# A hybrid SSD, RG-LRU, GLA and HGRN decoder step: transposes, scores, norm order and decay copies rearranged

## The chip, the cores and the metric

One core of one Trainium2 chip runs the whole program. The metric is the device time of one execution in microseconds (us). The kernel before took 1928.42 us, the median of 3 runs from 1928.1 to 1928.71 us.

## What is computed

Two layers of a decoder trunk on 592 tokens: 16 meta tokens, 8 sample sequences of 8 tokens, and a prompt of 512. Every product is in fp32.

```python
D_MODEL = 1024; D_FF = 4096; SEQ = 512; DEC_BATCH = 8; DEC_SEQ = 8; N_META = 16
# layer 0: 16 SSD heads (2 groups, head 64, state 128) and an RG-LRU (8 blocks of 128)
# layer 1: 4 GLA heads (key 128, value 256) and 8 HGRN heads (128, 128)
for layer in range(2):
    mixed = mixer(h)                       # one combined input projection, the heads, one output projection
    h = layer_norm(ALPHA * h + mixed)      # ln1
    h = layer_norm(ALPHA * h + square(relu(h @ w1)) @ w2)   # ln2
# SSD, per chunk:  y = (cb * decay) @ xd + (C @ S) * exp(b);   S = S * exp(b_last) + B.T @ (xd * to_end)
# GLA and HGRN:    scores = (q exp(b - b_ref)) @ (k exp(b_ref - b)).T, masked causal, times v, plus q exp(b) @ S
```

## The kernel before

Activations lie with features on partitions and tokens along the free axis: a tile "h" is one of eight slices of 128 features, 592 tokens wide, worked on in two halves of 296 (288 behind the last output projection). An fp32 product is made of three reduced-precision matmuls. `parts` casts a weight unit of 128x1024 to its high part on ScalarE (L126) and takes the low part by a subtraction on VectorE (L127); `mm` (L182) then runs k over the eight slices with three matmuls each, 24 matmuls for one 128x296 result in one of five PSUM banks ("pm"). `fast_pair` (L195) does half of the MLP's second product with fewer multiplications. Weight units are prepared three ahead of their use (`next_unit`, `prep_to`).

A `Task` is one weight unit with its result for both halves. The side work (heads, norms) is written as generators on a list `active`; `weave` advances each of them by one stage after every half task, and `later[k]` holds pieces that are to run inside the next product behind its k-th slice. So the order of the program text on the five engines comes from where a generator yields, and a scheduler settles the last details; every engine then executes its own instructions in order. The side work has three PSUM banks of its own ("px").

The parts that the change touches:

- **The norm** (class `Norm`). The last product in front of a norm has five slices without and three with the norm's sums woven in. `add` (L427 to L447) gives a slice's square to ScalarE (L446), adds it to the sum of squares "lnq" on VectorE (L447), and the slice itself to the sum "lns" (on POOL, for the last slice on VectorE, L444). `finishing` sums over partitions by two products with ones (L463, L465), makes the reciprocal deviation, subtracts the mean (L478), scales (L494) and writes the next layer's "h" as high part (ScalarE, L495) and low part (VectorE, L496). The first half's `finishing` starts inside the second half's first product behind slice FIK = 3; the second half's comes after everything that is pending has been drained.
- **The first product after a norm** runs its first four tasks by halves, each task with all of its k in turn (`run(..., by_half=True)`, L648 in the MLP; L1404 in the odd mixer, whose first task is a narrow one, L247).
- **The convolution** (`conv_task`, L689; 12 slices for SSD, 8 for RG-LRU): ScalarE moves the product out of PSUM into "pad" (L697 to L702), VectorE multiplies the first tap (L706) and adds the other three (L708 and the caller's).
- **An SSD pair** (`pair`, L831; 8 pairs of heads, two half tasks to a stage): POOL multiplies the log decays, high and low part, into a triangular mask (L843, 128x1024 each, and L845, 128x160 each); TensorE sums them along the chunk, ScalarE exponentiates (L881, L885). States follow (L903 to L925), "yi" = C S (L925) times its decay on VectorE, and then the outputs: L942 adds "yi" into the output bank as a product with the identity, L945 and L948 add the intra-chunk part.
- **A GLA or HGRN head** (`attend`): the decayed keys "kx" are laid out for four chunks of 128 tokens in three pieces of 64 (L1178 to L1203), and the scores are eight products of 64 columns (L1265, L1266), a full one of 128 keys for each half chunk of queries.

```python
            run([w1(0, f) for f in W1_ORDER[:4]], by_half=True)
    def finish(self, i, dst):
        if i == 0:
            later.setdefault(FIK, []).append(lambda: step(self.finishing(i, dst)))
```

## Time and profile before

| what | value |
|---|---|
| median of 3 runs | 1928.42 us |
| the profiled execution's own time | 1926.06 us |
| its span in the trace | 1924.3 us |
| mean granted TensorE clock | 0.987 of full speed |
| TensorE matmuls (PE) | 1858.2 us busy, 97% |
| VectorE (DVE) | 1297.1 us, 67% |
| ScalarE (ACT) | 886.0 us, 46% |
| GpSimd (POOL) | 417.2 us, 22% |

The profiled execution took 1.76 us more than its span, and 2.36 us less than the median of the three runs. The rows further down are from its trace. In a row of instructions the fields are the start in us, the time from the start of the first to the end of the last in us, engine, line, operation, output and inputs, shape and count; in brackets stands the time the engine idled before it and whose result ended the idling. A product in fp32 (all of L463, L942, L1265 and their like) appears as two matmul records, a reduced-precision one or a transpose as one. [...]

### The profile page before, as it was taken

The page shows a single profiled execution, that of the slowest core. Times are in us where ns is not written, and L with a number is a line of the kernel's source. Part 1 is how long each engine was busy: PE and PEld are TensorE (multiplying, and loading weights), DVE is VectorE, ACT ScalarE, POOL GpSimd, SP SyncE. Part 2 cuts the span into 40 slices and gives each one's busy share as a digit, 9 for nine tenths or more (in the row PEclk, how much of TensorE's full clock was granted, in tenths as well). Part 3 has the DMA queues.
Part 4 walks back from the last instruction along what each step waited for, and adds up shares of the span by engine and source line. Part 5 has one row for each costly group of instructions (what it writes and reads, how often), then busy time and mean ns, then how long its engine had stood idle before and what let it go on. Part 6 is the DMA issues. An engine that isn't in the chain of part 4 may idle for free.

```text
span 1924.3 us, 33593 instructions
## 1 busy us (share of the span) xinstructions
PE 1858.2 (97%) x13854; PEld 1819.0 (95%) x13854; DVE 1297.1 (67%) x2035; ACT 886.0 (46%) x1550; POOL 417.2 (22%) x435
## 2 busy tenths in 40 slices
PE   8998899999999999998999999999999999999996
PEld 8998799899999999998999999999999999999996
DVE  7997766877975756549645465665755976666647
ACT  5333246623644444324644455665732653534333
POOL 2554432214100000035422222221203200000024
PEclk9999899999999999999999999999999999999998
DMA  6232221421213131322332233223231214141311
GB/s 205 91 114 72 75 100 47 132 88 47 87 56 120 46 127 48 122 76 72 132 113 104 100 104 106 84 90 102 91 126 56 77 56 132 46 131 55 122 55 50
DMA packets 68761, 175.97 MB, mean 91 GB/s; under 512 B 6624, under 2 KB 30304, under 8 KB 67456
## 3 DMA queue, kind: packets, MB, share of 16 engines
q1 hardware_dynamic: 67968, 171.40, 26.5%
q8 instruction: 109, 1.79, 0.4%
q0 software_dynamic: 640, 2.43, 0.4%
q14 instruction: 44, 0.36, 0.1%
HBM read 154.54 MB, written 19.25 MB: 90 GB/s over the span
## 4 chain that ended last, share of the span: by engine, by line
PE 80%; DVE 13%; ACT 3%; issue 3%; POOL 0%; DMA 0%; SPq 0%; ACTq 0%; DVEq 0%; POOLq 0%
PE pm L182 55%; PE pm L195 14%; DVE w L127 1%; DVE r L424 1%; DVE h L496 1%; DVE r L494 1%; PE px L1326 1%; DVE r L478 1%; PE px L1337 1%; PE px L1336 1%; PE px L1067 1%; DVE lnq L447 1%; DVE acc L708 1%; PE px L925 1%; DVE ln L447 1%
## 5 line engine op out<-in xcount | busy, mean ns | idle before, releaser
L182 PE MATMUL pm<-h,w 128*128 128x296 f32 (+2 forms) x8256 | 1178.2, 301 | 11.0 <-ACT h L308 5.4
L182 PEld LDWEIGHTS pm<-h,w 128*128 128x128 f32 x8256 | 1132.6, 189 | 22.6 <-ACT h L308 5.4
L127 DVE TENSOR_TENSOR w<-raw,w 128x1024 fp32r<-128x1024 f32 (+1 forms) x300 | 369.7, 1233 | 165.1 <-ACT w L126 164.5
L126 ACT CAST w<-raw 128x1024 fp32r<-128x1024 f32 (+1 forms) x300 | 304.2, 1015 | 301.6 <-PE pm L195 152.2
L195 PE MATMUL pm<-ff,w 128*128 128x296 f32 (+1 forms) x2016 | 273.3, 297 | 0.0
L195 PEld LDWEIGHTS pm<-ff,w 128*128 128x128 f32 x2016 | 271.9, 188 | 0.1
L620 POOL TENSOR_TENSOR sq<-sq 128x296 f32<-128x296 f32 (+1 forms) x32 | 21.5, 674 | 651.4 <-ACT sq L618 651.4
L182 PE MATMUL pm<-m,w 128*128 128x296 f32 (+1 forms) x768 | 108.2, 304 | 0.0
L182 PE MATMUL pm<-ff,w 128*128 128x296 f32 (+1 forms) x768 | 108.0, 303 | 0.0
L182 PEld LDWEIGHTS pm<-m,w 128*128 128x128 f32 x768 | 106.8, 194 | 0.8 <-issue 0.3
L182 PEld LDWEIGHTS pm<-ff,w 128*128 128x128 f32 x768 | 106.6, 193 | 0.8 <-issue 0.3
L607 DVE TENSOR_TENSOR ff<-sq,ff 128x888 fp32r<-128x888 f32 (+3 forms) x48 | 58.4, 1221 | 42.1 <-ACT ff L606 42.1
L588 ACT ACTIVATE sq<-pm 128x296 f32<-128x296 f32 (+1 forms) x96 | 37.9, 414 | 87.0 <-PE pm L182 66.0
L606 ACT CAST ff<-sq 128x888 fp32r<-128x888 f32 (+3 forms) x48 | 50.3, 1050 | 39.6 <-DVE sq L601 38.9
L1361 POOL TENSOR_TENSOR o<-o,zs 128x576 f32<-128x576 f32 x16 | 31.3, 1967 | 148.7 <-DVE o L1360 148.7
L1280 POOL TENSOR_TENSOR sin<-sin,ebl 128x1024 f32<-128x1024 f32 (+1 forms) x12 | 35.8, 2980 | 106.1 <-issue 101.2
L211 DVE TENSOR_TENSOR r<-r,pm 128x296 f32<-128x296 f32 (+1 forms) x96 | 43.5, 453 | 18.6 <-PE pm L195 18.0
L589 ACT ACTIVATE sq<-sq 128x296 f32<-128x296 f32 (+1 forms) x96 | 41.2, 450 | 0.8
L1366 ACT COPY v<-pm 128x296 f32<-128x296 f32 x32 | 12.9, 405 | 58.6 <-PE pm L182 58.6
L214 DVE TENSOR_TENSOR r<-r,pm 128x296 f32<-128x296 f32 (+1 forms) x72 | 32.6, 452 | 10.2 <-PE pm L195 10.2
L618 ACT ACTIVATE sq<-pm 128x296 f32<-128x296 f32 (+1 forms) x32 | 13.0, 414 | 56.8 <-PE pm L182 53.8
L495 ACT ACTIVATE h<-r,vec 128x296 fp32r<-128x296 f32 (+1 forms) x48 | 23.8, 536 | 31.5 <-DVE r L494 31.5
(390 smaller groups left out, 2261.3 us busy)
## 6 DMA issues: line engine op xcount, KB each, us to landing
raw<-in_w_dram SPq DMA_DIRECT2D x252, 512.0 KB, 3.3
sin<-in_sst_dram SPq DMA_DIRECT2D x8, 512.0 KB, 3.7
out_ssd_s_dram<-sin SPq DMA_DIRECT2D x8, 512.0 KB, 3.1
sin<-in_gst_dram SPq DMA_DIRECT2D x4, 1024.0 KB, 5.7
out_gla_s_dram<-sin SPq DMA_DIRECT2D x4, 1024.0 KB, 3.9
sin<-in_hst_dram SPq DMA_DIRECT2D x8, 512.0 KB, 4.4
out_hgrn_s_dram<-sin SPq DMA_DIRECT2D x8, 512.0 KB, 3.5
xt<-in_x_dram SPq DMA_DIRECT2D x16, 148.0 KB, 4.2
```

What stands on the lines that cost most here:

```text
L126: A.copy(w[:, 0, :n], r)
L127: V.tensor_tensor(w[:, 1, :n], r, w[:, 0, :n].bitcast(F32), OP.subtract)
L182: PE.matmul(p[:, :n], w[:, a, ks], xs[k][:, b, c0:c1], start=(k == 0 and i == 0), stop=(k == KT - 1 and i == 2))
L195: PE.matmul(p[:, :n], w[:, a, ks], xs[k][:, b, :n], start=(first and k == 0 and i == 0), stop=(k == 3 and i == 2), skip_group_check=True)
L211: V.tensor_tensor(y, y, p[:, :n], OP.add)
L214: V.tensor_tensor(y, y, p[:, :n], OP.subtract)
L447: V.tensor_tensor(ss, ss, q, OP.add)
L588: A.activation(q, p, AF.Relu)
L589: A.activation(q, q, AF.Square)
L606: A.copy(t[:, 0, a:e, :n], s[:, a + 1:e + 1, :n])
L607: V.tensor_tensor(t[:, 1, a:e, :n], s[:, a + 1:e + 1, :n], t[:, 0, a:e, :n].bitcast(F32), OP.subtract)
L1280: G.tensor_tensor(sin, sin, ebl[:, 0:8].unsqueeze(2).to_broadcast([P, 8, N]), OP.mult)
```

## The change

Line numbers of the changed kernel are up to 53 higher. In six places:

1. A new function `together` takes the first four tasks behind a norm, opens their four PSUM banks at once and runs k on the outside: slice k is multiplied into all four results before slice k+1 is needed. The MLP's first four W1 tasks and the first GLA head's first four tasks use it for the first half; the second half runs in two groups of two.
2. In the norm the first half's `finishing` starts behind slice 6 instead of 3; the addition of a square waits until the next slice has been added (`add_square`); and before the second half's drain the next four weight units are prepared.
3. The convolution's first tap goes from VectorE (L706) to ScalarE, as an activation with scale and bias from a column.
4. The SSD log decays are no longer multiplied on POOL; ScalarE writes them as 20 copies for each pair with a scale per partition (16 of 128x128, 4 of 128x80), in three batches.
5. The product that adds "yi" into the outputs is marked as a transpose.
6. The scores are four products of 128 columns and four of 64 keys by 64 columns; "kx" becomes one run of 576 columns plus 256, so that the pieces of VectorE and ScalarE work around it are fewer; where a head has two value slices (GLA, `nv` == 2) the sample products move ahead of the scores.

```diff
 SHK = 5
-FIK = 3
+FIK = 6
 FINY = (2, 4, 6)
...
             self.consume(p, c0, c1, i)
+            flush()
+            weave()
+    def together(tasks, i):
+        ps = []
+        for t in tasks:
+            if t.small is None and t.w is None:
+                t.w = next_unit()
+            ps.append(pm())
+        for k in range(KT):
+            ks = slice(k * P, (k + 1) * P)
+            for t, p in zip(tasks, ps):
+                c0, c1 = t.halves[i]
+                if t.small is not None:
+                    ops = [(p[:32], t.small[:, k, :], b) for b in range(2)]
+                else:
+                    ops = [(p, t.w[:, a, ks], b) for a, b in ((0, 0), (0, 1), (1, 0))]
+                for j, (o, w, b) in enumerate(ops):
+                    PE.matmul(o[:, :c1 - c0], w, t.xs[k][:, b, c0:c1], start=(k == 0 and j == 0),
+                              stop=(k == KT - 1 and j == len(ops) - 1))
+            for fn in later.pop(k, ()):
+                fn()
+        for t, p in zip(tasks, ps):
+            c0, c1 = t.halves[i]
+            t.consume(p[:32 if t.small is not None else P, :c1 - c0], c0, c1, i)
             flush()
...
             self.new = new
+            self.square = None
...
             A.activation(q, r, AF.Square)
-            V.tensor_tensor(ss, ss, q, OP.add)
+            self.add_square()
+            self.square = (ss, q)
+        def add_square(self):
+            if self.square:
+                ss, q = self.square
+                V.tensor_tensor(ss, ss, q, OP.add)
+            self.square = None
...
             else:
+                prep_to(state["use"] + 4)
                 drain()
...
         def finishing(self, i, dst):
+            self.add_square()
             c0, c1 = self.halves[i]
...
-            run([w1(0, f) for f in W1_ORDER[:4]], by_half=True)
+            ts = [w1(0, f) for f in W1_ORDER[:4]]
+            together(ts, 0)
+            together(ts[:2], 1)
+            together(ts[2:], 1)
             for k, f in enumerate(W1_ORDER[4:]):
...
                 acc = cp.tile([P, PW], F32, tag="acc", name="acc")
-                V.tensor_scalar(acc[:, 0:OW], t[:, 0:OW], w(0), b, OP.mult, OP.add)
+                A.activation(acc[:, 0:OW], t[:, 0:OW], AF.Identity, scale=w(0), bias=b)
                 for k in (1, 2):
...
             rx = s1.tile([P, 2, 2, 80], F32R, tag="rx", name="rx")
-            for i, l in enumerate((lah.bitcast(F32), lal.bitcast(F32))):
-                G.tensor_tensor(rr[:, i], l[:, 1:5, hh].unsqueeze(3).to_broadcast([P, 4, 2, P]),
-                                umask[:, None, None, :].to_broadcast([P, 4, 2, P]), OP.mult)
-                G.tensor_tensor(rx[:, i], l[:, 0, hh].unsqueeze(2).to_broadcast([P, 2, 80]),
-                                uxmask[:, None, 0:80].to_broadcast([P, 2, 80]), OP.mult)
+            def decays(m):
+                for i, l in enumerate((lah.bitcast(F32), lal.bitcast(F32))):
+                    for h in range(2):
+                        def scaled(out, mask, c):
+                            A.activation(out, mask, AF.Copy, scale=l[:, c, 2 * j + h:2 * j + h + 1])
+                        if m == 2:
+                            scaled(rx[:, i, h], uxmask[:, 0:80], 0)
+                        else:
+                            for c in (2 * m, 2 * m + 1):
+                                scaled(rr[:, i, c, h], umask, c + 1)
+            decays(0)
             xr = s1.tile([P, 2, 3, 40], F32, tag="xr", name="xr")
...
             yield
+            decays(1)
+            decays(2)
             xd = s2.tile([P, 5, 2, 64], F32, tag="xd", name="xd")
...
                 PE.matmul(q[:, c * P:(c + 1) * P], yi[:, c].rearrange("p h q -> p (h q)"), ident,
-                          start=(c == 0), stop=False, skip_group_check=True)
+                          start=(c == 0), stop=False, is_transpose=True, skip_group_check=True)
             for h in range(2):
...
-            kx = sd.tile([P, 64 + 4 * 192], F32, tag="kx", name="kx")
-            kc = kx[:, 64:].rearrange("p (c r s) -> p c r s", c=4, r=3)
+            kx = sd.tile([P, 576 + 256], F32, tag="kx", name="kx")
+            k2 = kx[:, 576:].rearrange("p (c s) -> p c s", c=4)
             for o, s, r in zip(chunks(e1, 64), chunks(bs, 64), (4, 32)):
...
             b4 = chunks(bs, 128)[1]
-            V.tensor_tensor(kc[:, :, 1], b4[:, :, 96:97].to_broadcast([P, 4, 64]), b4[:, :, 0:64], OP.subtract)
+            V.tensor_tensor(k2, b4[:, :, 96:97].to_broadcast([P, 4, 64]), b4[:, :, 0:64], OP.subtract)
             c = slice(16, 592)
-            A.activation(kx[:, 0:64], e1[:, 16:80], AF.Exp, scale=-sc)
-            A.activation(kc[:, :, 0:3:2], e1[:, 80:592].rearrange("p (c r s) -> p c r s", c=4, r=2), AF.Exp, scale=-sc)
+            A.activation(kx[:, 0:576], e1[:, c], AF.Exp, scale=-sc)
             A.activation(e1[:, c], e1[:, c], AF.Exp, scale=sc)
             A.activation(e4, e4, AF.Exp, scale=sc)
-            A.activation(kc[:, :, 1], kc[:, :, 1], AF.Exp, scale=sc)
+            A.activation(k2, k2, AF.Exp, scale=sc)
             e3 = bs
...
             V.scalar_tensor_tensor(e1[:, c], q[:, c], qs, e1[:, c], OP.mult, OP.mult)
-            k4 = k[:, 80:592].rearrange("p (c r s) -> p c r s", c=4, r=2)
-            V.tensor_tensor(kx[:, 0:64], k[:, 16:80], kx[:, 0:64], OP.mult)
-            V.tensor_tensor(kc[:, :, 0:2], k4[:, :, 0:1].to_broadcast([P, 4, 2, 64]), kc[:, :, 0:2], OP.mult)
-            V.tensor_tensor(kc[:, :, 2], k4[:, :, 1], kc[:, :, 2], OP.mult)
+            V.tensor_tensor(kx[:, 0:576], k[:, c], kx[:, 0:576], OP.mult)
             V.tensor_tensor(e4, k, e4, OP.mult)
+            V.tensor_tensor(k2, chunks(k, 128)[1][:, :, 0:64], k2, OP.mult)
             for j in range(2):
...
+            u = px()
+            if nv == 2:
+                samples(u[:, 256:512])
             p = px()
...
                 a, b = ptiles(c + 1)
-                o = 64 + c * 192
-                PE.matmul(p[:, c * P:c * P + 64], kx[:, o:o + P], e1[:, a:a + 64], start=True, stop=True)
-                PE.matmul(p[:, c * P + 64:(c + 1) * P], kx[:, o + 64:o + 192], e1[:, a + 64:b], start=True, stop=True)
+                PE.matmul(p[:, c * P:(c + 1) * P], kx[:, a - 16:b - 16], e1[:, a:b], start=True, stop=True)
+            for c in range(4):
+                a, b = ptiles(c + 1)
+                PE.matmul(p[0:64, c * P + 64:(c + 1) * P], k2[:, c], e1[:, a + 64:b], start=True, stop=True)
             V.copy_predicated(scm[:, 0:512].rearrange("p (c n) -> p c n", n=P),
...
-            p = px()
-            if nv == 2:
-                samples(p[:, 256:512])
+            p = u
             for j in range(2):
...
             if h == 0:
-                run([Task(H, FULL, lr_consume, small=wsr[:, 1])] + tasks[0:NB], by_half=True)
-                run(tasks[NB:])
+                ts = [Task(H, FULL, lr_consume, small=wsr[:, 1])] + tasks
+                together(ts[:4], 0)
+                ts[4].half(0)
+                together(ts[:2], 1)
+                together(ts[2:4], 1)
+                ts[4].half(1)
             else:
...
             z = [g("zs"), g("zs")]
```

How the order moves, at three places. First TensorE at the end of layer 0's output projection and the start of its MLP ("m" the mixer's outputs, "h" the norm's, "lns" and "lnq" its two sums). Before:

```order
L182 MATMUL pm<-m_4615,w 128x296 x3
L182 MATMUL pm<-h,w 128x296 x25
L463 MATMUL px<-lns,ones 128x296
L465 MATMUL px<-lnq,ones 128x296
L182 MATMUL pm<-h,w 128x296 x455
L195 MATMUL pm<-ff,w 128x296 x324
```

and of the change:

```order
L182 MATMUL pm<-m_4743,w 128x296 x3
L311 MATMUL pm<-h,w 128x296 x32
L500 MATMUL px<-lns,ones 128x296
L311 MATMUL pm<-h,w 128x296 x7
L502 MATMUL px<-lnq,ones 128x296
L311 MATMUL pm<-h,w 128x296 x153
L182 MATMUL pm<-h,w 128x296 x288
L195 MATMUL pm<-ff,w 128x296 x324
```

The second half's sums (L463, now L500) stand behind 32 instead of 25 matmuls of the MLP, and those 32 use only the first three slices of "h" (12 for each slice), where the 25 used all eight.

Second, POOL over one SSD pair in the middle of the first group. Before:

```order
L868 TENSOR_TENSOR xdte<-xd,ex 128x512
L703 COPY pconv<-pad 128x3
L843 TENSOR_TENSOR rr<-lah,msk 128x1024
L845 TENSOR_TENSOR rx<-lah,msk 128x160
L843 TENSOR_TENSOR rr<-lal,msk 128x1024
L845 TENSOR_TENSOR rx<-lal,msk 128x160
L899 TENSOR_TENSOR sin<-sin,ex 128x1024
L695 MEMSET pad 128x3
```

and of the change:

```order
L919 TENSOR_TENSOR xdte<-xd,ex 128x512
L743 COPY pconv<-pad 128x3
L950 TENSOR_TENSOR sin<-sin,ex 128x1024
L735 MEMSET pad 128x3
```

The four products of the decays are gone from between the state products L868 and L899 (now L919 and L950).

Third, ScalarE over one SSD pair. Before:

```order
L881 ACTIVATE de<-px 128x512 x2
L885 ACTIVATE dx<-px 128x160
L697 COPY pad<-pm 128x16
L698 COPY pad<-pm 128x8x8
L699 COPY pad<-pm 128x216
L702 COPY pad<-pm 128x296
L126 CAST w<-raw 128x1024
L783 ACTIVATE pad<-acc 128x616
L984 ACTIVATE zs<-pm 128x296
L848 COPY xr<-xs 128x240
```

and of the change, in which L932 and L936 are the exponentials:

```order
L932 ACTIVATE de<-px 128x512 x2
L936 ACTIVATE dx<-px 128x160
L888 ACTIVATE rr<-msk,lah 128x128 x4
L888 ACTIVATE rr<-msk,lal 128x128 x4
L888 ACTIVATE rr<-msk,lah 128x128 x3
L823 ACTIVATE pad<-acc 128x616
L888 ACTIVATE rr<-msk,lah 128x128
L1035 ACTIVATE zs<-pm 128x296
L897 COPY xr<-xs 128x240
L888 ACTIVATE rr<-msk,lal 128x128 x4
L888 ACTIVATE rx<-msk,lah 128x80 x2
L888 ACTIVATE rx<-msk,lal 128x80
```

The twenty copies of a pair (L888) stand between the exponentials of the pair before and this pair's evictions from PSUM (L1035 "zs", before L984), one of them behind the eviction.

## Rows read from the trace of the kernel before

**Rows 1.** The page's first part, busy time, share and instructions of each engine.

```profile
PE 1858.2 (97%) x13854; PEld 1819.0 (95%) x13854; DVE 1297.1 (67%) x2035; ACT 886.0 (46%) x1550; POOL 417.2 (22%) x435
```

**Rows 2.** Waits of TensorE: releaser, us in total, times, longest.

```profile
PE px L918 <- DVE yi L897: 9.8, 3, 4.9
PE px L463 <- DVE ln L444: 8.2, 3, 3.5
PE px L463 <- DVE lns L444: 6.9, 2, 3.5
...
PE pm L182 <- DVE h L496: 3.0, 4, 1.1
PE px L1067 <- DVE xr L1055: 2.8, 1, 2.8
...
PE pm L247 <- DVE h L496: 1.7, 2, 1.3
```

**Rows 3.** SSD pair periods: length, busy us (records) of PE, PEld, DVE, ACT, POOL; clock; DMA.

```profile
81.02:102.04 21.02, 21.02 (x182) 20.14 (x182) 17.89 (x34) 6.82 (x15) 11.57 (x11) 1.00 0.29 103
...
152.20:182.12 29.92, 24.71 (x188) 23.10 (x186) 22.00 (x36) 10.04 (x20) 11.82 (x11) 0.89 0.22 78
182.12:209.38 27.26, 22.73 (x183) 21.56 (x181) 20.15 (x33) 6.72 (x15) 12.64 (x11) 0.94 0.21 70
209.38:238.29 28.91, 24.18 (x183) 23.00 (x182) 21.11 (x33) 6.59 (x13) 14.23 (x11) 0.88 0.21 72
```

**Rows 4.** Timeline of POOL in the last of these periods.

```profile
213.95 2.11 POOL L843 TENSOR_TENSOR rr<-lah,msk 128x1024 fp32r<-128x1024 f32 x1
```

**Rows 5.** Line 708: durations of one, min/median/max ns.

```profile
L708 DVE SCALAR_TENSOR_TENSOR acc<-pad,hcw,acc x24: 846/854/2514, 22.4 to 218.0; 128x616 f32<-128x616 f32 x24
```

**Rows 6.** Timeline of TensorE, products of 24 or 17 matmuls in and behind that period.

```profile
229.86 5.48 PE L182 MATMUL pm<-h,w 128*128 128x296 f32 x24
...
238.29 3.50 PE L182 MATMUL pm<-h,w 128*128 128x296 f32 x24
...
247.73 2.55 PE L182 MATMUL pm<-h,w 128*128 128x296 f32 x17
```

**Rows 7.** Lines 495 and 724 of ScalarE: durations, min/median/max ns.

```profile
L495 ACT ACTIVATE h<-r,vec x48: 522/537/547, 473.6 to 1525.4; 128x296 fp32r<-128x296 f32 x32, 128x288 fp32r<-128x288 f32 x16
...
L724 ACT CAST lsr<-msk x1: 322/322/322, 18.5 to 18.5; 128x128 fp32r<-128x128 f32 x1
```

**Rows 8.** Timeline of TensorE, outputs of one SSD pair.

```profile
140.85 1.10 PE L942 MATMUL px<-msk,yi 128*128 128x128 f32 x8
141.88 0.36 PE L945 MATMUL px<-dx,xd 128*64 128x80 f32 x4
```

**Rows 9.** Timeline of TensorE, four transposes of one SSD pair.

```profile
181.38 0.66 PE L857 MATMUL px<-msk,xs 128*128 128x128 f32 x4
181.87 0.27 PE L861 MATMUL px<-msk,xs 128*128 128x128 f32 x1
```

**Rows 10.** Timeline of TensorE, the scores of one head, first and last row.

```profile
952.38 0.33 PE L1265 MATMUL px<-e,kx 128*128 128x64 f32 x2
...
954.11 0.39 PE L1223 MATMUL px<-msk,v 128*128 128x128 f32 x2
```

**Rows 11.** Timeline of TensorE, eight products with 64 weight columns.

```profile
79.02 1.04 PE L948 MATMUL px<-de,xd 128*64 128x128 f32 x16
```

**Rows 12.** The 18 us behind the first and the last norm's first sums; columns as in rows 3.

```profile
463.60:482.30 18.70, 18.68 (x112) 18.06 (x113) 14.24 (x24) 10.38 (x17) 6.56 (x6) 0.83 0.25 83
1890.90:1909.20 18.30, 18.20 (x112) 17.38 (x112) 12.79 (x24) 7.26 (x16) 7.33 (x8) 0.85 0.19 65
```

**Rows 13.** Timeline of VectorE in the first norm.

```profile
460.27 0.70 DVE L447 TENSOR_TENSOR lnq<-lnq,lnu 128x296 f32<-128x296 f32 x1 [0.58 <-ACT lnu L446]
...
466.06 0.47 DVE L470 SCALAR_TENSOR_TENSOR lnr<-px,lnm 128x296 f32<-128x296 f32 x1 [2.03 <-PE px L465]
...
487.94 0.45 DVE L444 TENSOR_TENSOR lns<-lns,r 128x296 f32<-128x296 f32 x1
```

## The prediction

> **What bounds the kernel now.** The busy times come first: TensorE works 97% of the span, VectorE 67%, ScalarE 46%, GpSimd 22% [rows 1]. So a gain is either less TensorE work or one of the stretches in which TensorE waits or runs below its full clock; the three other engines matter only there. The list of TensorE's waits says where: the SSD outputs' banks (L918 behind VectorE's L897, 9.8 us in three waits), the norm's sums (L463 behind L444, 8.2 and 6.9 us in five), the first slices of the next layer's input (3.0 and 1.7 us behind L496), and one wait of 2.8 us in the RG-LRU stage [rows 2]. What a wait costs is more than its length, since the clock is down behind it: 24 matmuls took 3.50 us at full clock and 5.48 us behind such a wait; 17 took 2.55 us, so one more matmul is 0.136 us [rows 6].
>
> **SSD pairs: decays from POOL to ScalarE, first tap from VectorE to ScalarE.** An undisturbed pair lasts 21.02 us, all of them busy on TensorE [rows 3]. Three later periods last 29.92, 27.26 and 28.91 us at clocks of 0.89, 0.94 and 0.88 [rows 3]. The first of them has six matmuls more (188 against 182), 0.8 us. The excess is 8.1 + 6.2 + 7.9 = 22.2 us, and VectorE, busy 20 to 22 us in each, is what the waits name. Why is VectorE late? One of its convolution taps, 0.85 us as a rule, took 2.51 us at the latest start, 218.0 [rows 5], which is when POOL works through the decay products that began at 213.95 [rows 4]; the two engines slow each other. The change takes those four products from POOL, and the first tap from VectorE, some 0.6 us for each slice by the 0.85 us of the other taps, which read two tensors instead of one.
>
> ScalarE gets 20 copies and a tap for each pair. A plain cast of 128x128 took 0.322 us, an activation of 296 columns with scale and bias from columns 0.537 us [rows 7]; 20 times 0.32 is 6.4 us, and the tap of 616 columns, between these and the 0.85 us that VectorE needs for one, I put at 0.8 us. ScalarE is busy 6.6 to 10.0 us in a period [rows 3], so it comes to 14 to 17 of 21 us: the cover is there, though no longer wide, and it is gone only for a piece that TensorE needs at once. That piece exists: in the new order eleven or more copies (3.5 us) can stand ahead of an eviction. TensorE has five result banks and needs 3.3 us for one result, so a single such delay stays hidden. I take 18 of the 22.2 us; the ends are 10 (only the waits themselves and a part of the clock come back) and 22.
>
> **RG-LRU.** Its eight slices lose their first tap on VectorE too. One wait of 2.8 us behind VectorE's L1055 [rows 2]: 0 to 2.8 us, and I take all of it, since several taps of 0.6 us lie ahead of it.
>
> **The product with the identity as a transpose.** Its eight records take 1.03 us (140.85 to 141.88) [rows 8]; four transposes of the same shape, which are single records, take 0.49 us (181.38 to 181.87) [rows 9]. That is 0.54 us for each of 8 pairs, on the path: 4.3 us.
>
> **The scores.** Eight products took 1.73 us (952.38 to 954.11), 0.216 us each [rows 10]. Four remain full; the other four have 64 weight columns, as the SSD outputs' products have, of which eight (16 records) take 1.04 us, 0.13 us each [rows 11]. So 4 x 0.216 + 4 x 0.13 = 1.38 us, 0.35 us saved on a path where nothing waits, in 12 heads: 4.1 us. The lower end is 0, if a half-width product costs as much as a full one. The fewer pieces of "kx" work on VectorE and ScalarE lie beside TensorE's products; I cost them at nothing, since the heads show hardly a wait.
>
> **The norms.** There are four. In each, the first half's sums wait for L444; the waits of all, with one of the last norm's second half, add to 15.1 us, the longest 3.5 us [rows 2]. Three slices later is nine matmuls, 1.2 us of cover. The deferred addition of squares removes VectorE's idling for ScalarE's square, 0.58 us in one instance [rows 13] and three such in a row ahead of L444: 1.6 us. Of 3.5 us about 0.7 stay: 2.8 us gained, 11.2 us over four norms. Behind these waits the clock is at 0.83 and 0.85: 108 matmuls and the four records of the sums took 18.70 and 18.30 us [rows 12], where 108 x 0.136 and about 0.9 us for the sums make 15.6. That is up to 3 us each; with a wait of 0.7 us ahead most of it should return, but it need not, and I take 6 us for the four.
>
> The second half is where something comes back. From L470 (466.06) to the end of the second L444 (488.39) VectorE needs 22.3 us [rows 13], 20.7 without the idling. TensorE now has 99 matmuls of the projection and 32 of `together`, 131 x 0.136 = 17.8 us, until it stands at the second sums: a wait of about 2.9 us, at three norms 8.7 us, behind which all remaining tasks are queued. In exchange the waits for single slices go (3.0 + 1.7 us [rows 2]), since `together` uses a slice for 12 matmuls before it asks for the next. Sum for the norms: 11.2 + 6 - 8.7 + 4.7 = 13 us. The ends: 4, if the clock falls again behind the second sums; 24, if these are not late.
>
> **Sum.** 18 + 2.8 + 4.3 + 4.1 + 13 = 42 us off the profiled execution's 1926.06 us: 1884. The three runs' median lies 2.4 us above that execution, so 1886 us is the forecast. A measurement of this kernel can tell some 0.2%, 4 us, from no change.
>
> **Rivals.**
>
> *The norms give nothing* (13 becomes 0). The second sums' wait, and the low clock behind it, eat what the first sums return. For it: VectorE is the slower engine over the whole stretch, and moving its deadline does not make it shorter. Against it: 1.6 us of idling at each norm go in any case. 1886 + 13 = 1899 us.
>
> *VectorE stays late in the SSD pairs* (18 becomes 3). If its work of about 20 us in a period is set by its own length and not by POOL, or if the copies on ScalarE delay the exponentials, the same waits stay. For it: ScalarE executes in order and its copies stand ahead of others' evictions. Against it: the first pair's VectorE work, 17.89 us, fits into 21 [rows 3]. 1886 + 15 = 1901 us.
>
> *The cheaper TensorE forms cost what the old ones did* (8.4 becomes 0): 1894 us. For it, neither occurs in the program in just this place and accumulation; against it, the rows of both shapes.
>
> *The transposes let the clock fall.* Were the four transposes of a pair not work to the clock's gate, the product behind them would run as behind a wait: 5.48 for 3.50 us [rows 6], 8 x 2.0 = 16 us, so 1902 us. Against it: the period with seven transposes in front of its products (four, one and two) ran at 1.00 [rows 3]. [...]
>
> *Slower: ScalarE's queue becomes the bound of the SSD stage.* One mechanism: the copies of a pair are executed in one piece ahead of evictions and weight casts, the five result banks fill, and TensorE stands. It decides if more than three results wait at once, that is if ScalarE is more than some 10 us behind. Its price with half of the copies and taps exposed is 8 x 3.6 = 29 us, with nothing gained in the pairs: 1928.4 - 24 + 29 = 1933 us; with all exposed 1962 us. For it: eleven copies in a row. Against it: 14 to 17 us of work in 21.
>
> **How the numbers follow.** Forecast 0.52; norms give nothing 0.18; VectorE stays late 0.15; forms not cheaper 0.05; clock falls by transposes 0.02; ScalarE the bound 0.06; two of the gains missing together 0.02 (1914 us). The ends of the forecast itself are 1886 - (22 + 2.8 + 4.3 + 5.6 + 24 - 42) = 1869 us, where the scores save up to 5.6, and, with SSD 10 and the norms 4, 1886 + 17 = 1903 us. The range of 1867 to 1908 us takes in the first four cases and leaves the last two and the far ends out. Slower by over 0.2% is the fifth case in most of its course and some room for what I do not see: 0.06; within 0.2%: 0.04; faster: 0.90.
>
> **What would show it.** Right: no wait of TensorE above 1 us at L918's and L925's successors, pair periods of 21 to 22 us at a clock above 0.97, no VectorE tap above 1.1 us; ScalarE at 14 to 17 us in a period; the first sums waiting under 1 us and the second ones 2 to 4 us; 0.5 us for the four transposes; 1.4 us for a head's scores. Wrong: ScalarE named in TensorE's waits of the SSD stage; the clock at 0.9 behind the first sums as before; half-width products 0.2 us apart.

## The result and the profile after

The changed kernel took 1897.47 us, the median of four runs from 1896.57 to 1898.66, against 1928.26 us of the kernel before in the same comparison: a ratio of 0.9842, interval 0.9825 to 0.9859, 30.8 us less. The forecast was 1886 us with a range of 1867 to 1908 us. The profiled execution took 1896.57 us, its span is 1894.8 us (before 1926.06 and 1924.3).

The page's first part, after:

```profile
PE 1842.8 (97%) x13822; PEld 1802.8 (95%) x13822; DVE 1258.0 (66%) x2003; ACT 942.3 (50%) x1718; POOL 363.4 (19%) x403
```

Against [rows 1], TensorE has 15.4 us less to do, VectorE 39.1, POOL 53.8, and ScalarE 56.3 us more: the twenty copies of each pair and the twenty taps. TensorE's waits, after (releaser, us in total, times, longest):

```profile
PE pm L311 <- DVE r L556: 6.5, 4, 1.8
...
PE px L500 <- DVE ln L471: 4.4, 3, 1.5
PE pm L311 <- DVE r L671: 3.8, 2, 2.4
PE px L500 <- DVE lns L471: 2.9, 2, 1.5
PE px L1118 <- DVE xr L1106: 2.6, 1, 2.6
PE px L969 <- DVE yi L948: 2.5, 1, 2.5
PE pm L311 <- ACT sq L625: 2.4, 2, 1.3
```

Of [rows 2], the wait at the first member (L918, now L969) went from 9.8 to 2.5 us, and the norms' sums (L463, now L500) from 15.1 to 7.3. The RG-LRU wait (L1067, now L1118) stayed: 2.6 for 2.8. The waits for single slices went, and a new group came: L311, the four-bank product, waits 12.7 us, for "r" (VectorE empties the bank of the product before, L556 and L671) and for ScalarE's "sq".

Two pair periods of the first group and one of the second, after, columns as in [rows 3]:

```profile
73.89:95.24 21.35, 20.97 (x176) 19.72 (x176) 14.38 (x32) 13.17 (x36) 5.03 (x7) 1.00 0.28 102
95.24:116.63 21.39, 21.00 (x176) 19.75 (x176) 15.37 (x32) 13.18 (x36) 6.41 (x8) 1.00 0.28 102
...
195.09:216.92 21.83, 20.65 (x178) 19.67 (x178) 17.10 (x31) 13.06 (x36) 6.92 (x8) 1.00 0.31 102
```

The granted TensorE clock is 1.00, full speed, in all of them, the second group's periods fell from 27 to 30 us to 21.9, and VectorE needs 16 to 17 us where it needed 20 to 22. But the first group's, 21.02 us before, became longer: 21.35 and 21.39.

In the second group TensorE still waits for VectorE at the members that the prediction named, twice in these rows:

```profile
166.82 1.62 PE L969 MATMUL px<-xsr,bmx 120*128 120x128 f32 x8 [2.49 <-DVE yi L948]
...
212.49 1.13 PE L976 MATMUL px<-S,bc 128*128 128x128 f32 x8 [1.18 <-DVE S L962]
```

and one tap of VectorE (L821) is still stretched, from 0.85 to 2.52 us, beside a product of the state that POOL kept (L950). POOL, then VectorE:

```profile
206.13 2.23 POOL L950 TENSOR_TENSOR sin<-sin,ex 128x1024 f32<-128x1024 f32 x1 [4.17 <-PE px L945]
```

```profile
202.45 1.23 DVE L127 TENSOR_TENSOR w<-raw,w 128x1024 fp32r<-128x1024 f32 x1 [0.54 <-ACT w L126]
...
206.51 2.52 DVE L821 SCALAR_TENSOR_TENSOR acc<-pad,hcw,acc 128x616 f32<-128x616 f32 x1
```

Where the 29.5 us of the spans lie is read from the same instruction's start in both traces. The gain up to it, and what the stretch to it added:

| start of | before | after | gain so far | of this stretch |
|---|---|---|---|---|
| first pair's "yi" (L942, L993) | 77.81 | 73.89 | 3.9 | 3.9 |
| fourth pair's | 140.85 | 137.96 | 2.9 | -1.0 |
| eighth pair's | 256.61 | 237.70 | 18.9 | 16.0 |
| RG-LRU product behind its wait | 349.43 | 329.83 | 19.6 | 0.7 |
| first sums, norm 1 (L463, L500) | 463.62 | 443.41 | 21.4 | 1.8 |
| norm 2 | 875.54 | 854.66 | 22.1 | 0.7 |
| norm 3 | 1489.89 | 1464.97 | 26.1 | 4.0 |
| norm 4 | 1890.81 | 1866.17 | 25.8 | -0.3 |
| end | 1924.3 | 1894.8 | 29.5 | 3.7 |

In the four rows of the norms 1.2 us are added, since the first sums stand nine matmuls later in the changed kernel.

From the first pair's outputs to the eighth's, 15.0 us came back where the sum had put 22.3 (18 for the pairs, 4.3 for the transposes). The early stretch gave 3.9 us that stand in no term; 0.9 of them lie in the first 23 matmuls of the execution, whose time differs from trace to trace. The heads between norms 2 and 3 and the last norm gave something, and what lies behind the sums of norms 1 and 3 hardly anything.

### The profile page after: what moved, and what is told of

Read it like the earlier page. It is cut to its first block, busy times and chain, and to the rows that moved or that the text cites. A ratio compares the mean times of both kernels' runs of the same rounds, so it can differ in the third digit from the quotient of the medians.

```text
span 1894.8 us, 33652 instructions
## 1 busy us (share of the span) xinstructions
PE 1842.8 (97%) x13822; PEld 1802.8 (95%) x13822; DVE 1258.0 (66%) x2003; ACT 942.3 (50%) x1718; POOL 363.4 (19%) x403
## 4 chain that ended last, share of the span: by engine, by line
PE 81%; DVE 13%; ACT 3%; issue 2%; POOL 0%; DMA 0%; ACTq 0%; DVEq 0%
PE pm L182 54%; PE pm L195 14%; PE pm L311 2%; DVE w L127 2%; DVE r L515 1%; DVE r L531 1%; DVE h L533 1%; DVE r L451 1%; PE px L1375 1%; DVE acc L748 1%; PE px L1386 1%; PE px L1385 1%; PE px L1118 1%; ACT w L126 1%; PE px L1314 1%
## 5 line engine op out<-in xcount | busy, mean ns | idle before, releaser
L182 PE MATMUL pm<-h,w 128*128 128x296 f32 (+2 forms) x7728 | 1102.1, 301 | 6.2 <-ACT h L334 5.6
L311 PE MATMUL pm<-h,w 128*128 128x296 f32 (+1 forms) x528 | 82.7, 314 | 13.7 <-DVE r L556 6.5
L311 PEld LDWEIGHTS pm<-h,w 128*128 128x128 f32 x528 | 77.5, 200 | 18.2 <-ACT h L532 12.2
L1410 POOL TENSOR_TENSOR o<-o,zs 128x576 f32<-128x576 f32 x16 | 30.8, 1935 | 152.0 <-DVE o L1409 152.0
L211 DVE TENSOR_TENSOR r<-r,pm 128x296 f32<-128x296 f32 (+1 forms) x96 | 43.5, 453 | 18.8 <-PE pm L195 18.1
L1329 POOL TENSOR_TENSOR sin<-sin,ebl 128x1024 f32<-128x1024 f32 (+1 forms) x12 | 31.2, 2597 | 97.9 <-issue 93.1
L655 ACT ACTIVATE sq<-pm 128x296 f32<-128x296 f32 (+1 forms) x32 | 13.0, 414 | 56.8 <-PE pm L182 53.8
```

The lines of the kernel that those rows point to most:

```text
L182: PE.matmul(p[:, :n], w[:, a, ks], xs[k][:, b, c0:c1], start=(k == 0 and i == 0), stop=(k == KT - 1 and i == 2))
L211: V.tensor_tensor(y, y, p[:, :n], OP.add)
L311: PE.matmul(o[:, :c1 - c0], w, t.xs[k][:, b, c0:c1], start=(k == 0 and j == 0), stop=(k == KT - 1 and j == len(ops) - 1))
L1329: G.tensor_tensor(sin, sin, ebl[:, 0:8].unsqueeze(2).to_broadcast([P, 8, N]), OP.mult)
L1410: G.tensor_tensor(o[v][:, c], o[v][:, c], gate[v][:, c], OP.mult)
```

## The experiments

All kernels are the changed one with one edit unless said otherwise. "Ratio" is against the kernel before, with its interval; the change itself stands at 0.9842. The interval of a ratio is about 0.0015 to each side, 3 us, so smaller effects are read from the distance between the same two instructions in the traces. One caution there: the first 23 matmuls of an execution took 4.9 us in the change's trace and 4.8 to 6.0 us in others, which shifts everything behind them by up to 1.2 us, and single stretches behind a wait differ by some 1.6 us. Behind the same RG-LRU wait of 2.57 us, 24 matmuls take 5.19 us in the change's trace, where the granted clock is 0.50 from 332 to 334 us and 1.00 from 335 on, and 3.64 in e10's; behind the same wait of 2.49 us between the two groups of pairs, e8, whose edit does not reach that stage, needs 1.6 us more than the change.

| run | ratio | interval | median us |
|---|---|---|---|
| decays on POOL (e1) | 0.9929 | 0.9914 to 0.9944 | 1914.89 |
| extra POOL products (e2) | 0.9992 | 0.9983 to 1.0001 | 1926.70 |
| tasks by halves (e3) | 0.9823 | 0.9806 to 0.9839 | 1894.55 |
| old norm order (e4) | 0.9892 | 0.9877 to 0.9907 | 1908.21 |
| "yi" as a product (e5) | 0.9866 | 0.9849 to 0.9883 | 1903.64 |
| tap on VectorE (e6) | 0.9848 | 0.9833 to 0.9863 | 1899.22 |
| old scores (e7) | 0.9861 | 0.9847 to 0.9876 | 1901.84 |
| one more pause (e8) | 0.9824 | 0.9809 to 0.9838 | 1894.27 |
| extra POOL products on xs (e9) | 0.9859 | 0.9844 to 0.9873 | 1900.63 |
| subtractions on VectorE (e10) | 0.9797 | 0.9777 to 0.9817 | 1887.88 |
| both of the last two norm edits (e11) | 0.9788 | 0.9773 to 0.9802 | 1887.37 |
| the same, tasks by halves (e12) | 0.9792 | 0.9778 to 0.9807 | 1888.44 |

### The decays: does POOL slow VectorE?

e1 puts the four products back on POOL and keeps everything else:

```diff
-            decays(0)
+            for i, l in enumerate((lah.bitcast(F32), lal.bitcast(F32))):
+                G.tensor_tensor(rr[:, i], l[:, 1:5, hh].unsqueeze(3).to_broadcast([P, 4, 2, P]),
+                                umask[:, None, None, :].to_broadcast([P, 4, 2, P]), OP.mult)
+                G.tensor_tensor(rx[:, i], l[:, 0, hh].unsqueeze(2).to_broadcast([P, 2, 80]),
+                                uxmask[:, None, 0:80].to_broadcast([P, 2, 80]), OP.mult)
...
-            decays(1)
-            decays(2)
```

> The change, but with the SSD decays on POOL again. Contention theory (POOL's long products stretch VectorE's instructions): the three long pair periods come back with taps of 2.5 us, waits at the yi0 and state evictions of 2 to 5 us and a clock near 0.9; 14 to 19 us slower than the change, 1911 to 1917 us. Rival (VectorE was late by its own length, and the first tap's move alone cured it): within 4 us of the change, 1894 to 1901 us.

0.9929: 0.0087 above the change, 17 us, as the contention theory had it. The RG-LRU product starts at 347.03 instead of 329.83, so all of it lies in the SSD stage. VectorE in one pair of e1:

```profile
213.84 2.63 DVE L127 TENSOR_TENSOR w<-raw,w 128x1024 fp32r<-128x1024 f32 x1 [0.55 <-ACT w L126]
...
217.37 2.92 DVE L927 TENSOR_TENSOR de<-de,cbm 128x1024 f32<-128x1024 f32 x1
...
221.18 2.03 DVE L928 TENSOR_TENSOR dx<-dx,cbx 128x160 f32<-128x160 f32 x1
```

and POOL beside it:

```profile
213.49 1.91 POOL L884 TENSOR_TENSOR rr<-lah,msk 128x1024 fp32r<-128x1024 f32 x1
...
216.75 2.46 POOL L884 TENSOR_TENSOR rr<-lal,msk 128x1024 fp32r<-128x1024 f32 x1
```

VectorE's weight subtraction takes 2.63 us, the product "de" 2.92 and the short product "dx" 2.03, where the change's trace has 1.23, 1.22 and 0.32. This chain starts 7.36 us behind the outputs of the pair before in both traces (213.84 behind 206.48, 202.45 behind 195.09), so nothing ahead of it is late; its end, the next "yi" of VectorE, comes 17.42 us behind them in e1 and 13.86 in the change. TensorE's waits behind them are those of before, 2.4 and 2.3 us, and nobody waits for POOL. With the tap on ScalarE the same stall is there, so the tap's move did not cure it.

e2 was to add POOL work that nobody needs, eight products of 128x256 in each pair into a scratch tile:

```diff
+            dr = s1.tile([P, 2, P], F32, tag="dr", name="dr")
+            for i, l in enumerate((lah.bitcast(F32), lal.bitcast(F32))):
+                for c in range(4):
+                    G.tensor_tensor(dr, l[:, c + 1, hh].unsqueeze(2).to_broadcast([P, 2, P]),
+                                    umask[:, None, :].to_broadcast([P, 2, P]), OP.mult)
```

> The change with the decays on ScalarE as they are, plus eight POOL products of 128x256 in each pair into a scratch tile that nothing reads, at the place where the decay products stood (this adds work and alters no result). Contention theory: VectorE's instructions beside them stretch to 1.5 to 2.5 us again and the periods of the second group lengthen; 8 to 19 us slower than the change, 1905 to 1917 us, although nobody waits for these products. Rival (POOL's products mattered because their results came late): nothing waits for the scratch tile, so within 3 us of the change, 1894 to 1901 us.

The time rose by 29 us, but not for either reason. The products depend on nothing of their pair, so the scheduler placed all 64 between 45.8 and 102.3 us, ahead of the first pair's own POOL work, and TensorE waited for that:

```profile
67.71 1.12 PE L913 MATMUL px<-msk,xs 128*128 128x128 f32 x4 [7.83 <-DVE xs L827]
...
86.91 2.08 PE L963 MATMUL px<-xdte,btok 128*128 128x128 f32 x8 [11.94 <-POOL xdte L924]
```

The 11.94 us are for POOL's "xdte", queued behind the extra products; a third wait, 3.90 us, stands at 102.51. From the second pair on the periods are the change's. It shows what a filled queue costs, and says nothing of contention.

e9 lets the same products read the pair's own xs, so that they run in each pair:

```diff
+                    G.tensor_tensor(dr, l[:, c + 1, hh].unsqueeze(2).to_broadcast([P, 2, P]),
+                                    xs[:, 80:336].rearrange("p (h t) -> p h t", h=2), OP.mult)
```

> The change, the decays on ScalarE as they are, plus eight POOL products of 128x256 in each pair into a scratch tile that nothing reads; they now read the pair's own xs, so that they run in every pair and not ahead of the first (this adds work and alters no result). Contention theory: VectorE's taps and subtractions beside them take 1.5 to 2.5 us instead of 0.85 to 1.2, and with some 5.5 us of such products in each pair the periods of the second group grow by 1 to 5 us each: 4 to 15 us slower than the change, 1901 to 1912 us, with VectorE named in TensorE's waits. Rivals: POOL's queue (the products stand ahead of xdte), then POOL's xdte is named; or no effect, within 3 us of the change, 1894 to 1901 us.

0.9859, 3.3 us above the change: below the range of the contention theory, at the edge of the other. The trace says why it is so little. VectorE:

```profile
100.50 0.69 DVE L914 TENSOR_TENSOR xd<-px,dt 128x512 f32<-128x512 f32 x1
...
106.67 2.53 DVE L127 TENSOR_TENSOR w<-raw,w 128x1024 fp32r<-128x1024 f32 x1
109.12 1.63 DVE L942 TENSOR_TENSOR de<-de,cbm 128x1024 f32<-128x1024 f32 x1
```

POOL:

```profile
100.24 2.00 POOL L899 TENSOR_TENSOR dr<-lah,xs 128x256 f32<-128x256 f32 x3
...
106.65 1.46 POOL L1013 TENSOR_TENSOR sq<-sq 128x592 f32<-128x592 f32 x1
108.06 1.60 POOL L899 TENSOR_TENSOR dr<-lal,xs 128x256 f32<-128x256 f32 x1
```

The product xd, one of whose inputs ("px") lies in PSUM, is not stretched: 0.69 us, 0.68 to 0.69 in the change's trace, though POOL is busy from 100.24 to 102.24. The weight subtraction, both of whose inputs lie in SBUF, is: 2.53 us, and "de" 1.63, where the change's trace has 1.23 and 1.22; and POOL's own product beside them takes 1.60 us instead of 0.61. Of this pair's eight extra products four began while VectorE read PSUM and two while it was idle. In the first group "yi" comes 1.0 us later and the periods grow from 21.35 to 22.32 us; in the second group they stay at 21.85. But the 1.0 us are no proof of contention. ScalarE's "sq" waits for POOL's "y", which now stands behind extra products, and the copies, the eviction and the tap behind it on ScalarE come late with it. The change, then e9:

```profile
121.95 0.70 ACT L1005 ACTIVATE sq<-y 128x592 f32<-128x592 f32 x1 [3.01 <-POOL y L1003]
```

```profile
104.39 0.70 ACT L1010 ACTIVATE sq<-y 128x592 f32<-128x592 f32 x1 [5.22 <-POOL y L1008]
```

That is the rival of POOL's queue, in another place than expected. So e9 shows contention in the durations, with what it took here (a VectorE instruction with both inputs in SBUF at the same time as POOL's product), and e1 shows what it cost in time.

### The tap and the transposes

e6 returns the first tap of the convolution to VectorE:

```diff
-                A.activation(acc[:, 0:OW], t[:, 0:OW], AF.Identity, scale=w(0), bias=b)
+                V.tensor_scalar(acc[:, 0:OW], t[:, 0:OW], w(0), b, OP.mult, OP.add)
```

> The change with the convolution's first tap on VectorE again. Delay theory (on ScalarE the tap stands behind a weight cast, so yi and xs come about 0.8 to 1.0 us later in a pair): the pair periods of the first group fall from 21.35 to 20.5 us, and the time is 1 to 4 us below the change, 1893 to 1896 us. Rival (as predicted, VectorE is too full for the tap): the waits of the second group and the RG-LRU wait of 2.6 us grow, 2 to 6 us slower, 1899 to 1903 us.

0.9848, which cannot be told from the change. The parts go opposite ways. The first group's periods fall to 21.02 to 21.10 us (from 21.33 to 21.39), and the one from the fifth pair to the sixth from 21.90 to 20.80: 2.0 us over four periods. The first group's do not fall to 20.5, because there TensorE is busy 20.61 of 21.03 us and waits 0.42 for xs; the shorter transposes let it arrive before xs is ready. The step between the groups grows by 1.5 us (36.74 for 35.23), and the stretch from the RG-LRU product to the first norm by 1.2 (114.77 for 113.58; the wait 2.86 for 2.57 us). Both of these lie in the stretch behind a wait, where the change's trace has the clock at 0.50 (168 to 170 us, 332 to 334 us), the first of them behind a wait of the same length, and are no larger than what traces with the change's tap differ by. So the tap on ScalarE costs 2.0 us in the pairs, and a gain from it elsewhere is not shown. Why it costs there stands on ScalarE's and VectorE's rows of the change:

```profile
89.84 0.41 ACT L742 COPY pad<-pm 128x296 f32<-128x296 f32 x1 [0.84 <-PE pm L182]
90.14 1.05 ACT L126 CAST w<-raw 128x1024 fp32r<-128x1024 f32 x1
91.09 0.90 ACT L746 ACTIVATE acc<-pad,hcb,hcw 128x616 f32<-128x616 f32 x1
```

```profile
92.36 0.85 DVE L748 SCALAR_TENSOR_TENSOR acc<-pad,hcw,acc 128x616 f32<-128x616 f32 x1
...
94.50 0.68 DVE L980 TENSOR_TENSOR yi<-px,ex 128x512 f32<-128x512 f32 x1
...
96.82 0.91 DVE L827 SCALAR_TENSOR_TENSOR xs<-pad,acc 128x16 f32<-128x16 f32 x3 [0.86 <-ACT pad L823]
```

The tap (L746) waits on ScalarE behind the weight cast that starts at 90.14, and VectorE's chain of taps, with "yi" (L980) in the middle, begins at 92.36. "yi" ends at 95.18, and TensorE waits 0.17 us for it; xs ends at 97.73.

e5 takes the mark of the transpose away:

```diff
-                          start=(c == 0), stop=False, is_transpose=True, skip_group_check=True)
+                          start=(c == 0), stop=False, skip_group_check=True)
```

> The change with L993 as a plain fp32 product again. Direct theory (as predicted): 0.54 us more for each of 8 pairs, 4.3 us slower than the change, span 1899.1 against 1894.8 us. Rival (in the first group's pairs TensorE waits for VectorE's xs right behind, 0.2 us each with a drained pipeline, and in the second for S): the longer product fills those waits, 0 to 2.5 us slower, pair periods of the first group 21.3 to 21.5 us as now and the xs waits gone.

0.9866, 4.6 us above the change. The RG-LRU product starts 6.2 us later, 1.0 of it from the first 23 matmuls; the periods grow by 0.4 us in the first group and 0.4 to 0.6 in the second, 2.7 us over six periods or 3.6 for eight pairs at that rate, and the step between the groups (140.20 to 177.42 us) by 2.0; in it lies again the stretch behind a wait, in which traces differ by some 1.6 us. Beside the change the direct theory holds nearly in full: the waits for "yi" and xs hide little. (Three more us of e5's span lie between norms 3 and 4, which this edit does not reach.)

### The scores

e7 has the old layout of "kx" and the eight full products:

```diff
-                PE.matmul(p[:, c * P:(c + 1) * P], kx[:, a - 16:b - 16], e1[:, a:b], start=True, stop=True)
-                PE.matmul(p[0:64, c * P + 64:(c + 1) * P], k2[:, c], e1[:, a + 64:b], start=True, stop=True)
+                PE.matmul(p[:, c * P:c * P + 64], kx[:, o:o + P], e1[:, a:a + 64], start=True, stop=True)
+                PE.matmul(p[:, c * P + 64:(c + 1) * P], kx[:, o + 64:o + 192], e1[:, a + 64:b], start=True, stop=True)
```

> The change with the eight full score products and the old layout of kx. Theory (the half-width products are cheaper where nothing waits): 0.35 us for each of 12 heads, 4.1 us slower, span about 1898.9 us, and the scores of one head take 1.73 us against about 1.4. Rival (a half-width product costs as much, or the saving falls into another wait): under 1 us of difference, and then the 4 us between the second and the third norm come from that norm.

0.9861; from norm 2 to norm 3 615.07 us against the change's 610.31: 4.8 us. One head's scores in the change, and what follows:

```profile
1164.55 1.05 PE L1314 MATMUL px<-e,kx 128*128 128x128 f32 x8
1165.54 0.68 PE L1317 MATMUL px<-e,kx 128*64 128x64 f32 x8
1166.14 0.65 PE L1325 MATMUL px<-sin,qm 128*32 128x128 f32 x16
```

They take 1.59 us (1164.55 to 1166.14) in each head, 1.82 in e7's eight HGRN heads and 1.73 in its four GLA heads: 0.23 and 0.14 us, 2.4 us in all and less than the 0.35 of the sum for each head, because the four full products of 128 columns take 0.25 us each and the half-width ones 0.15. The rest is elsewhere in the head: between the meta tokens' score product and the transposes of "kst" e7 needs 0.42 us (1195.95 to 1196.37) and the change 0.17 (1195.17 to 1195.34); the last six HGRN heads show such a difference, 0.16 to 0.42 us. Nothing but the "kx" pieces on VectorE and ScalarE differs there, which I had costed at nothing.

### The norms

e4 returns the old order (FIK 3, squares at once, no preparation ahead of the drain):

```diff
-FIK = 6
+FIK = 3
...
-            self.add_square()
-            self.square = (ss, q)
+            V.tensor_tensor(ss, ss, q, OP.add)
...
-                prep_to(state["use"] + 4)
```

> The change, but the first half's sums behind slice 3 again, squares added at once and no weight units prepared ahead of the drain. If the norm order is what returned the full clock behind the first sums: waits of 3.5 us and a clock of 0.83 to 0.90 behind them at four norms, 12 to 20 us slower than the change, 1909 to 1917 us. Rival (the later start only moves the wait to the banks behind it): 0 to 6 us slower, 1897 to 1903 us, most of it at the last norm.

e3's edit at the MLP (the first GLA head's tasks likewise go back):

```diff
-            together(ts, 0)
-            together(ts[:2], 1)
-            together(ts[2:], 1)
+            run([w1(0, f) for f in W1_ORDER[:4]], by_half=True)
```

> The change, but the first tasks behind a norm run one after the other by halves again (no function together). Bank theory (opening four result banks at once waits for VectorE's evictions and gives back what the slice order saves): the 10 us of waits of the four-bank products on VectorE's r vanish, the waits for single slices and the second sums come back at about the same size, and the time is within 4 us of the change, 1894 to 1901 us. Rival (the slice order is worth the 4.7 us of slice waits and the clock behind them at three norms): 5 to 12 us slower, 1902 to 1909 us.

The distance from one norm's first sums to the next one's, in us (the sums of the kernel before and of e4 stand nine matmuls earlier, which shows only in the last column, as 1.2 us):

| run | norm 1 to 2 | 2 to 3 | 3 to 4 | 4 to end |
|---|---|---|---|---|
| before | 411.92 | 614.35 | 400.92 | 33.49 |
| the change | 411.25 | 610.31 | 401.20 | 28.63 |
| by halves (e3) | 410.65 | 610.30 | 400.58 | 28.66 |
| old order (e4) | 413.68 | 610.46 | 406.02 | 32.21 |
| one more pause (e8) | 409.94 | 609.90 | 400.52 | 28.87 |
| subtractions on VectorE (e10) | 407.87 | 607.25 | 399.28 | 27.62 |
| both (e11) | 407.87 | 610.40 | 397.61 | 27.60 |
| both, by halves (e12) | 407.82 | 607.26 | 399.46 | 27.60 |

e3 is 0.6 us shorter at two norms and equal elsewhere; by the ratio it is 3.7 us below the change, with intervals that overlap. So `together` is worth nothing here, as the bank theory had it. The order is worth some 10 us beside it: 2.4, 0.2 and 4.8 in the first three stretches and, less the 1.2, 2.4 in the last. That lies between the two theories of e4, and the 4.8 are not all safe: e5, which does not touch the norms, is 3.0 us longer in the same stretch. TensorE behind the first norm's first sums, in the change:

```profile
443.41 0.77 PE L500 MATMUL px<-lns,ones 128*128 128x296 f32 x2 [1.52 <-DVE lns L471]
...
444.29 13.92 PE L182 MATMUL pm<-m,w 128*128 128x296 f32 x99
...
460.77 1.32 PE L311 MATMUL pm<-h,w 128*128 128x296 f32 x8 [1.60 <-DVE r L556]
463.85 4.21 PE L311 MATMUL pm<-h,w 128*128 128x296 f32 x18 [1.76 <-DVE r L556]
467.90 0.66 PE L500 MATMUL px<-lns,ones 128*128 128x296 f32 x2
```

The first sums wait 1.52 us, the clock is not lost behind them (99 matmuls in 13.92 us, granted clock 1.00 from 443.40 to 460.80), and the second sums do not wait at all. But the four-bank product stops twice, 1.60 and 1.76 us, for a bank that VectorE has not emptied, and the clock falls behind that second stop: 18 matmuls take 4.21 us, and from there to 475.00 the granted clock is 0.85 in the mean, 0.50 from 465 to 467 us and 1.00 from 468 on (columns as in [rows 3]):

```profile
463.85:475.00 11.15, 11.15 (x67) 10.91 (x68) 9.96 (x16) 2.47 (x7) 5.09 (x5) 0.85 0.15 48
```

VectorE over the same time:

```profile
445.17 0.46 DVE L556 TENSOR_TENSOR r<-r,pm 128x296 f32<-128x296 f32 x1
...
448.17 4.12 DVE L515 TENSOR_TENSOR r<-r,lnt 128x296 f32<-128x296 f32 x4
452.22 1.21 DVE L127 TENSOR_TENSOR w<-raw,w 128x1024 fp32r<-128x1024 f32 x1
...
457.99 0.45 DVE L556 TENSOR_TENSOR r<-r,pm 128x296 f32<-128x296 f32 x1
...
460.17 0.45 DVE L556 TENSOR_TENSOR r<-r,pm 128x296 f32<-128x296 f32 x1
...
463.25 0.45 DVE L556 TENSOR_TENSOR r<-r,pm 128x296 f32<-128x296 f32 x1
```

It empties one bank at 445.17 and the next only at 457.99, 460.17 and 463.25, with the slices of "h" and three weight subtractions in between. What stands out is the row at 448.17: four mean subtractions of 128x296 in 4.12 us, 1.03 each, while POOL does the other four.

e8 gives VectorE one pause more, so that a bank is emptied ahead of the third slice:

```diff
-FINY = (2, 4, 6)
+FINY = (0, 2, 4, 6)
```

> The change with one more pause in the norm, ahead of the first slice (FINY = 0, 2, 4, 6), so that VectorE empties the projection's result banks one slice pair earlier. Bank theory: the waits of the four-bank products for VectorE's r, 10.3 us at three norms, fall by more than half, 3 to 6 us faster than the change, 1891 to 1894 us. Rival (VectorE as a whole is the bound between the first and the second sums, so the slices come as much later as the banks come earlier): within 2 us of the change, the waits only change their names.

0.9824: 3.5 us by the ratio, with intervals that overlap; by the table 1.3, 0.4 and 0.7 us. At the first norm the waits changed places (2.42 us once instead of 1.60 and 1.76): VectorE as a whole is late.

e10 therefore shortens VectorE's work by giving it more of it, all eight subtractions:

```diff
-SUBP = (1, 3, 5, 7)
+SUBP = ()
```

> The change with the norm's eight mean subtractions all on VectorE (SUBP empty) instead of four on VectorE beside four on POOL. Contention theory: the four beside POOL took 4.1 us, eight alone take 8 x 0.45 = 3.6 us, so the eight halves of the norms end 0.5 us earlier each; the tail behind the last sums shortens by 0.3 to 0.5 us and the norms' stretches by 0 to 1.5 us each, 1 to 4 us faster than the change, 1893 to 1896 us. Rival (POOL does carry half of the work): VectorE needs 8 us instead of 4, 3 to 10 us slower, 1900 to 1907 us.

0.9797, interval 0.9777 to 0.9817, apart from that of the change: 8.7 us less, twice what was expected at most. VectorE and TensorE in e10's first norm:

```profile
447.64 1.59 DVE L515 TENSOR_TENSOR r<-r,lnt 128x296 f32<-128x296 f32 x4
...
450.28 1.59 DVE L515 TENSOR_TENSOR r<-r,lnt 128x296 f32<-128x296 f32 x4
...
455.54 0.46 DVE L556 TENSOR_TENSOR r<-r,pm 128x296 f32<-128x296 f32 x1
...
458.65 0.45 DVE L556 TENSOR_TENSOR r<-r,pm 128x296 f32<-128x296 f32 x1
```

```profile
459.15 2.74 PE L311 MATMUL pm<-h,w 128*128 128x296 f32 x18 [0.52 <-DVE r L556]
462.24 2.72 PE L311 MATMUL pm<-h,w 128*128 128x296 f32 x18 [0.34 <-DVE r L556]
465.19 0.77 PE L500 MATMUL px<-lns,ones 128*128 128x296 f32 x2 [0.23 <-DVE lns L471]
```

Alone, four subtractions take 1.59 us, eight 3.2; the change's four took 4.12. The next two banks are emptied at 455.54 and 458.65, 2.0 and 1.0 us earlier once the 0.5 us are taken off by which this trace is ahead, and the waits fall to 0.52, 0.34 and 0.23 us. About half of the first of these gains, 0.9 us, is order: the bank is emptied behind two low parts of "h" in e10 and behind four in the change. With the waits this short the clock stays up, 1.00 from 459.20 to 477.00: 18 matmuls take 2.74 and 2.72 us where 18 took 4.21. So e10's gain is both the shorter waits (1.1 us in all for 3.4) and the clock behind them. The table's row gives 3.4, 3.1, 1.9 and 1.0 us for the four norms.

e11 takes both of these edits, and e12 e3's tasks as well:

```diff
-FINY = (2, 4, 6)
+FINY = (0, 2, 4, 6)
...
-SUBP = (1, 3, 5, 7)
+SUBP = ()
```

> The subtractions all on VectorE and the extra pause of FINY = 0, 2, 4, 6 together, with the four-bank products of the change. If VectorE's length between the first and the second sums is the bound, both add: 3 to 7 us faster than the change, 1890 to 1894 us. If the extra pause only renamed the waits and the subtractions are neutral: within 3 us of it, 1894 to 1900 us.

> As the run before, but with the tasks behind a norm one after the other by halves instead of the four-bank products. If the banks are what the four-bank products pay for, this is the fastest of all, 1889 to 1893 us; if the earlier evictions already free the banks, the slice order is worth something now and this run is 1 to 4 us slower than the one with both, 1891 to 1897 us.

e11 has 0.9788 and e12 0.9792: neither can be told from e10 or from each other. (In e11's stretch from norm 2 to 3, 610.40 us, TensorE waits 2.90 us once for ScalarE's "q", 0.35 in e10.) So the extra pause and the slice order add nothing that these runs can show once VectorE has the time; the one edit of e10 is the version to keep, 1887.88 us, 40 us below the kernel before and about 9 below the change.

## Why the prediction came out as it did

- **The sum: in the range, and partly by luck.** The sum of 42 us became 29.5 us between the two spans: 7.9 us less than forecast at the norms, 3.4 less in the SSD stage with the early stretch counted in, 2.1 less at RG-LRU, 0.7 more at the scores. The 3.9 us of the early stretch (waits of 1.5 and 1.9 us at 44 and 51 us before, 0.4 and 0.2 after) had no term in the sum; without them the time would have been about 1901 us, next to the rivals at 1899 and 1901.
- **The pairs: right in the cause, short in size.** 18 us were taken. e1 undoes the decays alone and loses 15.3 us between the fourth pair's outputs and the eighth's (115.03 us for 99.74), with VectorE's stretched rows. (The tap of 2.51 us in [rows 5] stands at 186.73; the last one, at 218.0, took 2.50. Both lie beside the decay products.) Part of what was to go stayed: waits of 2.49, 1.23 and 1.18 us at L969 and L976, where none above 1 us was expected, and a tap of 2.52 us beside POOL's L950, where none above 1.1 was. ScalarE, 13.2 us busy in a period of 21.35 (14 to 17 were expected), kept its cover, and it is named only once in TensorE's waits of the stage (0.6 us). So the slower rival's condition did not arise.
- **The tap: wrong sign in the pairs.** It was counted as a relief alone. It put a step on ScalarE, behind a weight cast, into the chain that ends in "yi" and xs, and cost 2.0 us over four periods (e6).
- **RG-LRU: wrong.** All 2.8 us were taken; the wait fell by 0.24 us. The step that failed is that "several taps of 0.6 us lie ahead of it". Before, only one first tap, 0.57 us at 344.31, stands right ahead of the wait's end. In the change's trace VectorE has scans, gate products and two weight subtractions ahead of the taps without a gap, and the finished first tap lies waiting from 323.9 to 326.9 us.
- **The transposes: priced right, gained in part.** 4.3 us expected; e5 shows 3.6 in the periods, and in the change's trace a pair's four take 0.53 us (173.19 to 173.72). But the first group's periods did not become shorter than before: what TensorE saved there became waits for "yi" and xs. And from the fourth pair to the eighth e1, which has the transposes and the moved tap, gains only 0.7 us on the kernel before. The rival that the clock would fall by them did not come: the periods ran at 1.00 with four more transposes in each, eleven in all. (At 1902 us this rival, too, lay in the range, which the prediction does not say.)
- **The scores: right in sum, 4.1 expected and 4.8 in e7**, but only 2.4 us came from the products. The sum priced the four full ones at 0.216 us, which [rows 10] show for 64 columns; with 128 columns they take 0.25, and the half-width ones 0.15 for 0.13. The rest fits the "kx" pieces that were costed at nothing.
- **The norms: the largest part of what is missing.** 13 us were expected, some 5 came: 1.8 up to the first sums, 0.7, -0.8 (with the scores' 4.8 taken off) and -0.3 in the three stretches behind, 3.7 at the end. The first steps held in part: the first sums wait 1.5 us (3.5 before, 0.7 expected), and the clock behind them stays up, at 1.00 behind the first norm's. The step that failed is the one on the second half, which let `together` use "a slice for 12 matmuls before it asks for the next" and left only "a wait of about 2.9 us" at the second sums. At the first three norms those wait for nothing; what is late is the emptying of the banks, four of five at once, by a VectorE that is busy throughout, and behind these waits the clock falls after all, at the first norm to 0.50 from 465 to 467 us and 0.85 in the mean of 11.15 us. That is the rival "the norms give nothing" in its reason, VectorE as the slower engine over the whole stretch; e10 shows it by shortening VectorE's work and getting 8.7 us. At the last norm no product needs a bank that is emptied late, and there the forecast's mechanism gave its gain, though the second sums still wait 1.4 us (1.2 before).

What stays open: why the old order costs so unequally beside the four-bank products (0.2 us in the stretch behind norm 2, 4.8 behind norm 3); how much of that is the clock's recovery was not separated. Nor was it separated how much of e10's gain is the clock and how much the shorter waits.

## What to carry to other kernels

In this kernel work halved between VectorE and POOL, both reading SBUF, was not done in half the time: four subtractions beside POOL took 4.1 us, eight alone 3.2 (e10), so try the undivided version first. When a wait is removed, price the whole of the engine that produced it up to the next point at which it is needed; a deadline that moves without its work getting shorter turns up as the next wait, here at the PSUM banks. An order that needs many result banks at once depends on whoever empties them (here two waits for VectorE, 1.60 and 1.76 us, at the first norm).

## What the runs showed of the hardware that was not expected

VectorE and POOL delayed each other, and where the operands lay made a difference: with both inputs in SBUF a VectorE instruction took 2.53 us for 1.23 and POOL's beside it 1.60 for 0.61, while one that read PSUM kept its 0.69 us (e9). The mutual delay was longer than doing both in turn: 4.12 us beside POOL in the change against 2 x 1.59 alone (e10).
